# Ten steps of the samples' matrix memory ahead of the heads in place of eight, in a decoder step whose order is written out

## The chip, the cores and the metric

The kernel runs on one core of one Trainium2 chip. The metric is device time in microseconds (us) of one execution, lower is better; the median of the runs of the kernel before is 1042.33 us (1041.23 to 1043.42, three runs). The engines are TensorE (PE), with its weight loads shown apart as PEld, VectorE (DVE), ScalarE (ACT), GpSimd (POOL) and SyncE (SP), which issues nearly all transfers.

## The reference, cut to what matters

One step of a decoder trunk of two layers, in float32: 512 new tokens of a prompt and one new token for each of 8 samples share the weights. Layer 0 is a native sparse attention, layer 1 an mLSTM of 4 heads of width 512. The change concerns layer 1: its gate path z, and the part of the mLSTM that updates each sample's matrix memory C of 512 x 512, one for each of 8 samples and 4 heads, so 32 in all.

```python
# nsa layer: q, k, v, gates, z = h @ w_in; three branches (compressed, selected, window); out = (o * silu(z)) @ w_out
# mLSTM layer:
proj = h @ w_in
xm, z = proj[..., :D_INNER], proj[..., D_INNER:]          # D_INNER = 2048
c = jax.nn.silu(conv)                                      # conv of xm, width 4
q, k, v = block products of c and xm; ig, fl = gates of q, k, v
# per sample and head, one token:
num   = S @ v + decay * (q @ C)
den   = sum(S) + decay * (q . n)
hc    = num / max(|den|, exp(-mt))
C_new = carry_decay * C + w * outer(k, v)                  # 512 x 512, an output
hn    = hc * rsqrt(mean(hc * hc) + eps)
out   = (hn * norm_w + skip * c) * jax.nn.silu(z)
return x + out @ w_out
```

The prompt's 512 tokens go through the same cell, as one chunk of decay weights here.

## The kernel before, in words

The 520 tokens lie along the free axis and are worked in two column halves of 260. Every product in float32 is made as three products of rounded parts, high by high, high by low and low by high; so each weight tile is loaded (`wraw`), rounded to its high part (`whi`, on ACT or DVE) and subtracted to its low part (`wlo`, on DVE or POOL), before PE can use it.

By the time at which PE works on them, the stages of the profiled execution are: key, value and compression 0 to 207 us; q and z of layer 0 to 307; attention to 467; the product with W_o to 518; the xm half of layer 1's input product to 647; the zm stage, that is the z half, to 751; the heads to 996; the last output product and norm to 1036.

No scheduler decides the order. Each stage first registers its operations with their dependences, and then emits them in the sequence that a table of numbers gives: ORDER0 for the attention (934 operations), CALLS1 for the 712 recorded pieces of W_o and xm, ORDER1 for the zm stage (348 operations) and ORDER2 for the heads (933). Each engine runs what it is given strictly in that order. A second kind of table, MOVED1 for the pieces of CALLS1 and MOVEDP0 to MOVEDP2 for the other three, names operations that change engine: a copy between ACT and DVE, an elementwise operation between DVE and POOL. All instructions are emitted by one helper, so every row of the profile has its line, L504, and rows are told apart by the tiles they write and read.

The zm stage takes the 15 remaining of 16 weight tiles of z (`wraw<-in_m_in`, 512 KB each), one product for each half of the columns (24 matmuls `mm<-hhi,whi` and the like), its SiLU and a store (`zd<-zt`). Beside this it works out the prompt's gates, and runs the first eight steps of the samples' memory. A step k is sample k % 8 of head k // 8 (`state_step`):

- two loads of half a memory each (`cs<-in_state_C`, 512 KB);
- on PE the read of the old memory, 8 small matmuls `d<-cs,QZ`, gathered over the 8 samples of a head in one bank `d`, and one matmul `t<-VB,OH` that spreads the sample's v over the partitions;
- on ACT two multiplications by the decay (`cs<-cs,SBC`), on DVE four outer products added to it (`cs<-t,wk,cs`);
- two stores `o_cs<-cs`, 512 KB each.

Ahead of a head's first step `head_open` makes the samples' q for it (`QZ`), its rows and `VB`; after its eighth step `head_close` takes the denominators (`sd`, `dn`, `nm`), squares the result (`pr`) and sums the squares on PE with `t<-pr,ones`, and normalises it into `HN`. NZ says how many steps stand in the zm stage:

```python
    for ft in range(1, 16):
        zm_ops(P, ft, ZT * (ft - 1))
    gate_ops(P, GDUE)
    for k in range(NZ):
        state_step(P, k, ZS0 + ZSP * k)
    for n in range(2 * NZ, 2 * NZ + 4):
        state_load(P, n, ZT * 15 - 10)
    P.run(ORDER1, R, NE, MOVEDP1)
```

The remaining steps stand in the heads, among the prompt's heads: for each head the values v are split in high and low parts (`vh`, `vl`), q and k are made by block products (`mm<-CT,bdm`, `t<-bdk,ctw`), scores `s<-q,CT` follow, then the values, the head's norm (`acc`, `hx`, `hy`), the gating into `num`, its split in `uh` and `ul`, and 8 output products of 4 tiles each (`mm<-uh,whi` and the like, out_unit), each added to the residual `x`.

Of the kernel before, what the change touches and what calls it, by code (L numbers as in the profile page):

```python
# [55 lines left out]
ZT, ZS0, ZSP, NZ, GDUE = 6.4, 6.0, 11.0, 8, 8.0  # L56
# [52 lines left out]
)  # L109
ORDER1 = (  # L110
# [16 lines left out]
)  # L127
ORDER2 = (
# [173 lines left out]
MOVEDP1 = (7, 27, 31, 42, 46, 47, 61, 77, 82, 87, 91, 112, 117, 127, 132, 136, 162, 166, 167, 172, 177, 181, 182, 192,  # L302
    196, 197, 202, 211, 212, 248, 255,)
# [237 lines left out]
def step_kernel(ctx, tc, ap):  # L541
# [1409 lines left out]
    xm_val(15)  # L1951
    R.run(NE, CALLS1, MOVED1)
    mctx.close()
# [912 lines left out]
```

## Time and profile before

| | before |
|---|---|
| median of three runs | 1042.33 us |
| the profiled execution | 1037.7 us |
| its span | 1036.0 us |
| mean granted PE clock | 0.998 |
| PE busy | 1012.9 us, 98% of the span |
| DVE busy | 784.4 us, 76% |
| ACT busy | 532.7 us, 51% |
| POOL busy | 380.6 us, 37% |
| moved by DMA | 197.19 MB, mean 190 GB/s |

Busy time is the time in which an engine has an instruction in work. Matmuls overlap in PE's pipeline and their ends are modelled, so that a row's mean of 285 ns for a matmul of 260 columns is longer than the 0.12 us that lie between the starts of two. A wait is the idle time of an engine just before an instruction, put down to what released it. The profiled execution's own time is 4.6 us below the median of the runs shown.

### The profile page before, as it was taken

The numbers are of one execution on the slowest core, as the hardware profiler recorded it, in microseconds if no ns is written. First come the engines' busy times: TensorE is split into PE (matmuls) and PEld (weight loads), VectorE is DVE, ScalarE is ACT, GpSimd is POOL, SyncE is SP. The second block draws the span as 40 slices with busy tenths as digits, with TensorE's granted clock in tenths as the row PEclk, the third lists the DMA queues.
The fourth block names the chain that finished last, engine by engine and source line by source line (L and its number), as shares of the span: only waits on it lengthen the run. The fifth ranks groups of instructions, "written<-read, shape, count | busy, mean of one in ns | idle before, by whom it ended". The sixth has DMA issues, their size and how long they took to land.

```text
span 1036.0 us, 24026 instructions
## 1 busy us (share of the span) xinstructions
PE 1012.9 (98%) x8743; PEld 909.0 (88%) x8743; DVE 784.4 (76%) x1879; ACT 532.7 (51%) x1228; POOL 380.6 (37%) x430
## 2 busy tenths in 40 slices
PE   7999999999999999999999999999999999999998
PEld 6989999899998888779999998898857678877987
DVE  7876764568568987775887786866677888989885
ACT  5253342533268877761444455656655665463543
POOL 1072433301246656362234433332323335434330
PEclk9999999999999999999999999999999999999999
DMA  7664453133335624547434642688789789898543
GB/s 251 200 199 143 152 163 121 50 117 118 113 100 159 188 84 123 164 144 255 144 110 166 209 144 73 245 277 304 276 269 358 256 273 316 284 338 287 190 137 113
DMA packets 124793, 197.19 MB, mean 190 GB/s; under 512 B 16118, under 2 KB 66167, under 8 KB 124419
## 3 DMA queue, kind: packets, MB, share of 16 engines
q1 hardware_dynamic: 118866, 186.37, 54.7%
q10 hardware_dynamic: 5808, 9.28, 2.5%
q8 instruction: 69, 1.13, 0.4%
q14 instruction: 50, 0.40, 0.1%
HBM read 145.89 MB, written 58.10 MB: 197 GB/s over the span
## 4 chain that ended last, share of the span: by engine, by line
PE 67%; DVE 5%; ACT 2%; POOL 1%; issue 0%; DMA 0%; ACTq 0%; DVEq 0%
PE mm L504 44%; PE s L504 9%; PE t L504 8%; PE d L504 6%; ACT s L504 1%; DVE num L504 1%; DVE s L504 1%; POOL s L504 0%; DMA wraw<-in_m_in 0%; DVE ul L504 0%; DVE x L504 0%; ACT pt L504 0%; DVE wlo L504 0%; DVE hx L504 0%; DVE sc L504 0%
## 5 line engine op out<-in xcount | busy, mean ns | idle before, releaser
L504 PE MATMUL mm<-hhi,whi 128*128 128x260 f32 (+1 forms) x952 | 273.1, 287 | 0.9 <-ACT hhi L504 0.9
L504 PE MATMUL mm<-hhi,wlo 128*128 128x260 f32 (+1 forms) x952 | 269.9, 283 | 2.1 <-POOL wlo L504 1.1
L504 PE MATMUL mm<-hlo,whi 128*128 128x260 f32 (+1 forms) x952 | 269.6, 283 | 0.0
L504 PEld LDWEIGHTS mm<-hhi,whi 128*128 128x128 f32 (+1 forms) x952 | 178.4, 187 | 5.6 <-issue 3.6
L504 PEld LDWEIGHTS mm<-hhi,wlo 128*128 128x128 f32 (+1 forms) x952 | 178.3, 187 | 2.8 <-DVE wlo L504 1.5
L504 PEld LDWEIGHTS mm<-hlo,whi 128*128 128x128 f32 (+1 forms) x952 | 178.1, 187 | 0.8 <-DVE hlo L504 0.2
L504 POOL TENSOR_TENSOR wlo<-wraw,whi 128x1024 fp32r<-128x1024 f32 (+2 forms) x49 | 94.5, 1931 | 177.1 <-DVE whi L504 118.1
L504 DVE SCALAR_TENSOR_TENSOR cs<-t,wk,cs 128x512 f32<-128x512 f32 x128 | 89.1, 743 | 13.0 <-ACT cs L504 11.3
L504 ACT ACTIVATE cs<-cs,SBC 128x1024 f32<-128x1024 f32 x64 | 71.6, 1144 | 33.8 <-PE d L504 31.2
L504 POOL TENSOR_SCALAR s<-s,sm 128x256 f32<-128x256 f32 (+3 forms) x69 | 70.1, 1026 | 38.6 <-DVE sm L504 20.2
L504 ACT ACTIVATE s<-s,mn 128x256 f32<-128x256 f32 (+3 forms) x128 | 70.6, 554 | 16.8 <-DVE mn L504 12.8
L504 PE MATMUL s<-phi,w1h 128*128 128x256 f32 (+1 forms) x256 | 77.1, 301 | 0.0
L504 PE MATMUL s<-plo,w1h 128*128 128x256 f32 (+1 forms) x256 | 74.7, 292 | 2.3 <-DVE plo L504 2.3
L504 PE MATMUL s<-phi,w1l 128*128 128x256 f32 (+1 forms) x256 | 74.1, 289 | 0.0
L504 DVE TENSOR_TENSOR wlo<-wraw,whi 128x1024 fp32r<-128x1024 f32 (+1 forms) x53 | 61.1, 1154 | 9.2 <-ACT whi L504 4.5
L504 ACT ACTIVATE whi<-wraw 128x1024 fp32r<-128x1024 f32 (+1 forms) x53 | 46.7, 884 | 38.8 <-DMA wraw<-in_m_out 14.1
L504 PE MATMUL mm<-uh,whi 128*128 128x260 f32 x224 | 65.1, 291 | 0.0
L504 PE MATMUL mm<-uh,wlo 128*128 128x260 f32 x224 | 63.3, 282 | 1.5 <-DVE wlo L504 1.5
L504 DVE CUSTOM_DVE_ANT_0 s<-s,D 128x512 f32<-128x512 f32 (+3 forms) x128 | 57.8, 488 | 7.8 <-PE s L504 7.4
L504 PE MATMUL mm<-ul,whi 128*128 128x260 f32 x224 | 63.2, 282 | 0.0
L504 PEld LDWEIGHTS s<-plo,w1h 128*128 128x128 f32 x256 | 48.4, 189 | 4.0 <-DVE plo L504 2.8
L504 PEld LDWEIGHTS s<-phi,w1h 128*128 128x128 f32 x256 | 48.3, 189 | 0.6
(481 smaller groups left out, 2623.4 us busy)
## 6 DMA issues: line engine op xcount, KB each, us to landing
cs<-in_state_C SPq DMA_DIRECT2D x64, 512.0 KB, 6.5
o_cs<-cs SPq DMA_DIRECT2D x64, 512.0 KB, 5.0
praw<-in_cache SPq DMA_DIRECT2D x128, 128.0 KB, 3.0
dk<-in_cache SPq DMA_DIRECT2D x128, 128.0 KB, 2.6
wraw<-in_m_in SPq DMA_DIRECT2D x32, 512.0 KB, 4.0
wraw<-in_m_out SPq DMA_DIRECT2D x32, 256.0 KB, 4.9
wraw<-in_w_kv SPq DMA_DIRECT2D x11, 512.0 KB, 3.7
wraw<-in_w_q SPq DMA_DIRECT2D x8, 512.0 KB, 3.8
```

The costliest lines, as they stand in the source:

```text
L504: return f(*[real(x) for x in a], **{n: real(x) for n, x in k.items()})
```

## The change

NZ goes from 8 to 10. Steps 8 and 9, the first two samples of head 1, and with them the `head_open` of head 1, are registered in the zm stage and no longer in the heads: 25 operations, so that the zm stage has 373 and the heads 908. ORDER0, ORDER1, ORDER2 and CALLS1 are replaced as a whole, as are MOVED1 and MOVEDP0 to MOVEDP2; operations that change engine are 123 in place of 118 in the attention, 136 in place of 139 in W_o and xm, 38 in place of 31 in the zm stage and 111 in place of 116 in the heads. CALLS0, CALLS2, CALLS3 and their tables are as before. No operation is added or taken away.

```diff
--- before.py
+++ after.py
-ZT, ZS0, ZSP, NZ, GDUE = 6.4, 6.0, 11.0, 8, 8.0
+ZT, ZS0, ZSP, NZ, GDUE = 6.4, 6.0, 11.0, 10, 8.0
 ORDER0 = (
-    828, 792, 54, 55, 57, 834, 830, 8, 9, 108, 10, 11, 13, 14, 12, 71, 15, 37, 28, 793, 16, 17, 59, 60, 34, 61,
...
+    911, 830, 828, 792, 54, 55, 8, 13, 9, 10, 834, 11, 12, 71, 14, 15, 16, 17, 37, 28, 31, 61, 59, 57, 793, 18,
...
-MOVED1 = (20, 27, 29, 30, 36, 45, 52, 61, 62, 69, 71, 72, 73, 79, 88, 89, 95, 104, 112, 117, 126, 127, 152, 157, 164,
...
+MOVED1 = (27, 29, 30, 36, 45, 46, 59, 67, 68, 72, 73, 79, 88, 89, 95, 105, 117, 124, 126, 127, 147, 152, 157, 164,
...
-MOVEDP0 = (19, 20, 23, 24, 41, 47, 64, 65, 66, 67, 69, 84, 93, 95, 99, 119, 120, 123, 164, 166, 167, 184, 186, 190,
...
-MOVEDP1 = (7, 27, 31, 42, 46, 47, 61, 77, 82, 87, 91, 112, 117, 127, 132, 136, 162, 166, 167, 172, 177, 181, 182, 192,
...
-MOVEDP2 = (82, 94, 170, 177, 189, 265, 272, 284, 285, 286, 288, 292, 295, 309, 338, 346, 357, 362, 373, 387, 388, 389,
...
+MOVEDP0 = (7, 19, 20, 23, 24, 41, 47, 50, 64, 66, 69, 84, 86, 89, 93, 95, 98, 99, 119, 120, 124, 164, 167, 184, 186,
...
+MOVEDP1 = (1, 12, 16, 22, 32, 42, 52, 57, 62, 76, 77, 82, 87, 92, 97, 102, 106, 117, 121, 127, 136, 142, 147, 152,
...
+MOVEDP2 = (57, 145, 152, 240, 247, 257, 258, 262, 263, 267, 282, 291, 294, 296, 313, 321, 322, 326, 332, 336, 337,
...
```

First place: PE where the zm stage ends and the heads begin. `t<-sd,ncs`, `t<-pr,ones` and `t<-cst,lse` belong to the closing of head 0 and to the gates, `d<-cs,QZ` and `t<-VB,OH` to steps of the memory, `mm<-CT,bdm` to the prompt's q. Before:

```order
L504 MATMUL mm<-hhi_9105,wlo 128x260
L504 MATMUL t<-sd,ncs 32x8 x16
L504 MATMUL t<-pr,ones 32x64 x4
L504 MATMUL t<-cst,lse 128x128 x4
L504 MATMUL t<-pr,ones 32x32 x4
L504 MATMUL t<-cst,VS 8x128 x4
L504 MATMUL mm<-CT_9799,bdm 128x512
L504 MATMUL mm<-CT_9898,bdm 128x512
L504 MATMUL mm<-CT_9950,bdm 128x512
L504 MATMUL d<-cs,QZ_10218 32x512 x8
```

The changed kernel, in the same place:

```order
L504 MATMUL mm<-hlo_9193,whi 128x260
L504 MATMUL mm<-hhi_9072,wlo 128x260
L504 MATMUL t<-VB,OH 128x512
L504 MATMUL d<-cs,QZ_9877 32x512 x4
L504 MATMUL t<-cst,lse 128x128 x4
L504 MATMUL t<-VB,OH 128x512
L504 MATMUL t<-pr,ones 32x32 x4
L504 MATMUL t<-VB,OH 128x512 x2
L504 MATMUL d<-cs,QZ_9877 32x512 x4
L504 MATMUL mm<-CT_9799,bdm 128x512
L504 MATMUL mm<-CT_9724,bdm 128x512
```

The sums `t<-sd,ncs` and `t<-pr,ones` 32x64 now stand some 100 instructions further up (outside the piece), ahead of the last four half tiles of z; `t<-pr,ones` 32x32 has the memory read of step 9 and two spreads around it, and the block products of q come behind two more spreads and the read of step 10. The read that follows `mm<-CT,bdm` before is that of step 8, which now stands inside the last tile of z.

The same place on DVE, from the denominators `dn` and `nm` of head 0 over `pr` to the sum of squares `dn<-t` and the factor `hf_v`; `zt` is the SiLU of z. Before:

```order
L504 TENSOR_TENSOR zt<-mm,rr_9636 128x260
L504 TENSOR_REDUCE dn<-t 128x16
L504 TENSOR_TENSOR dn<-dn,SBC 128x16
L504 TENSOR_TENSOR dn<-dn 128x8
L504 TENSOR_TENSOR zt<-zt,zsg_12598 128x260
L504 TENSOR_TENSOR dn<-dn,SBC 128x8
L504 RECIPROCAL dn<-dn 128x8
L504 TENSOR_TENSOR nm<-VS,dn 128x32
L504 TENSOR_TENSOR nm<-nm,t 128x32
L504 TENSOR_TENSOR pr<-nm 128x32
L504 TENSOR_REDUCE dn<-t 128x8
L504 TENSOR_TENSOR hf_v<-dn 128x8
```

The changed kernel:

```order
L504 TENSOR_TENSOR nm<-VS,dn 128x32
L504 TENSOR_TENSOR nm<-nm,t 128x32
L504 TENSOR_TENSOR pr<-nm 128x32
L504 TENSOR_TENSOR zt<-zt,zsg_12517 128x260
L504 TENSOR_TENSOR zt<-zt,zsg_12559 128x260
L504 TENSOR_TENSOR zt<-mm,rr_9555 128x260
L504 TENSOR_TENSOR zt<-mm,rr_9632 128x260
L504 SCALAR_TENSOR_TENSOR cs<-t,wk,cs 128x512 x8
L504 TENSOR_REDUCE dn<-t 128x8
L504 TENSOR_TENSOR hf_v<-dn 128x8
L504 TENSOR_TENSOR hf_v<-hf_v,dn 128x8
```

`pr` came directly before the sum of its squares; now four rows of the SiLU and the eight outer products of steps 8 and 9, in one row here, stand between them.

Second place: the transfers that SP issues at the start of the zm stage, in this order (the numbers are those of the tiles). Before:

```order
L504 DMA wraw_11303<-in_m_in 128x1024
L504 DMA wraw_11334<-in_m_in 128x1024
L504 DMA wraw_11342<-in_m_in 128x1024
L504 DMA cs_11346<-in_state_C 128x2x512
L504 DMA cs_11391<-in_state_C 128x2x512
L504 DMA cs_11456<-in_state_C 128x2x512
L504 DMA zd_8938<-zt_11406 128x512
L504 DMA wraw_11518<-in_m_in 128x1024
```

The changed kernel:

```order
L504 DMA wraw_11310<-in_m_in 128x1024
L504 DMA wraw_11325<-in_m_in 128x1024
L504 DMA wraw_11356<-in_m_in 128x1024
L504 DMA cs_11358<-in_state_C 128x2x512
L504 DMA wraw_11373<-in_m_in 128x1024
L504 DMA cs_11443<-in_state_C 128x2x512
L504 DMA cs_11450<-in_state_C 128x2x512
L504 DMA wraw_11452<-in_m_in 128x1024
L504 DMA cs_11494<-in_state_C 128x2x512
```

Three weight tiles are still issued ahead of the first memory loads; the fourth (`wraw_11373`) now comes next and serves z tile 5, and the fifth (`wraw_11452`) serves tile 4, whose product comes first. Its buffer is that of `whi` of tile 2, which PE has to have read before.

Third place: DVE in the last of the four heads, where the head's norm ends and the gating begins. `hx<-t,hx` reads the head's sum of squares from PE, `num` is the gating, `x<-x,mm` the residual of an output product, `cs<-t,wk,cs` an outer product of the last steps. Before:

```order
L504 TENSOR_TENSOR pr<-nm 128x32
L504 TENSOR_TENSOR x_13211<-x_13211,mm 128x260 x2
L504 SCALAR_TENSOR_TENSOR hx<-t,hx 128x512
L504 TENSOR_REDUCE dn<-t 128x8
L504 TENSOR_TENSOR hf_v<-dn 128x8
L504 TENSOR_TENSOR hf_v<-hf_v,dn 128x8
L504 TENSOR_SCALAR hf_v<-hf_v 128x8
L504 TENSOR_TENSOR x_14009<-x_14009,mm 128x260
L504 TENSOR_TENSOR hx<-hx,hy 128x512 x2
L504 SCALAR_TENSOR_TENSOR hy<-hx,hy 128x512
L504 TENSOR_TENSOR wlo<-wraw,whi 128x512
```

The changed kernel:

```order
L504 SCALAR_TENSOR_TENSOR hx<-hx,ab 128x512
L504 TENSOR_TENSOR acc<-acc,sq_15208 128x512
L504 TENSOR_TENSOR wlo<-wraw,whi 128x512
L504 CAST whi<-wraw 128x512
L504 SCALAR_TENSOR_TENSOR cs<-t,wk,cs 128x512 x2
L504 SCALAR_TENSOR_TENSOR hx<-t,hx 128x512
L504 TENSOR_TENSOR x_13682<-x_13682,mm 128x260 x2
L504 TENSOR_REDUCE dn<-t 128x8
L504 TENSOR_TENSOR hf_v<-dn 128x8
L504 TENSOR_TENSOR hf_v<-hf_v,dn 128x8
L504 TENSOR_SCALAR hf_v<-hf_v 128x8
L504 TENSOR_TENSOR hx<-hx,hy 128x512 x2
```

A row of the sum `acc`, two of weight splits and two outer products now stand directly ahead of `hx<-t,hx`.

More of the change, by code (lines that the diff above doesn't have):

```diff
@@ L295 @@
 MOVED3 = (2, 12, 16, 23, 30, 31, 35, 42, 65, 69, 103, 120, 124, 136, 141,)
-MOVEDP0 = (19, 20, 23, 24, 41, 47, 64, 65, 66, 67, 69, 84, 93, 95, 99, 119, 120, 123, 164, 166, 167, 184, 186, 190,
[5 rows of a table removed]
-MOVEDP1 = (7, 27, 31, 42, 46, 47, 61, 77, 82, 87, 91, 112, 117, 127, 132, 136, 162, 166, 167, 172, 177, 181, 182, 192,
-    196, 197, 202, 211, 212, 248, 255,)
-MOVEDP2 = (82, 94, 170, 177, 189, 265, 272, 284, 285, 286, 288, 292, 295, 309, 338, 346, 357, 362, 373, 387, 388, 389,
[5 rows of a table removed]
+MOVEDP0 = (7, 19, 20, 23, 24, 41, 47, 50, 64, 66, 69, 84, 86, 89, 93, 95, 98, 99, 119, 120, 124, 164, 167, 184, 186,
[5 rows of a table added]
+MOVEDP1 = (1, 12, 16, 22, 32, 42, 52, 57, 62, 76, 77, 82, 87, 92, 97, 102, 106, 117, 121, 127, 136, 142, 147, 152,
+    157, 162, 177, 182, 187, 192, 211, 212, 222, 225, 230, 246, 248, 328,)
+MOVEDP2 = (57, 145, 152, 240, 247, 257, 258, 262, 263, 267, 282, 291, 294, 296, 313, 321, 322, 326, 332, 336, 337,
[5 rows of a table added]
 LATE = ((3, 1), (3, 2), (3, 3))
```

302 rows, old and new, of tables (CALLS1, MOVED1, MOVEDP0, MOVEDP2) are left out of this document.

## The prediction

> **What bounds the kernel now.** I read the busy times by stage first, then the waits of PE, then the chain of waits and the timelines at the two ends of the moved work. The busy times of each engine in the attention, the zm stage and the heads (columns: PE, PEld, DVE, ACT, POOL, each with its count, then the granted clock, the DMA engines' share and GB/s):
>
> ```profile
> 307.00:467.00 160.00, 159.01 (x1902) 132.19 (x1899) 131.81 (x517) 122.00 (x377) 92.14 (x107) 0.99 0.48 143
> 647.00:751.00 104.00, 101.70 (x858) 92.72 (x851) 73.77 (x134) 62.61 (x119) 33.23 (x40) 1.00 0.79 276
> 751.00:996.00 245.00, 242.74 (x1748) 188.71 (x1746) 211.63 (x463) 131.44 (x221) 91.66 (x102) 1.00 0.83 282
> ```
>
> PE is busy for 101.70 of 104 us in the zm stage and 242.74 of 245 in the heads, at full clock. So PE bounds both, and since the change adds and removes no matmul, the time can fall only by what PE waits for. All the waits of PE that matter (us in total, times, longest):
>
> ```profile
> PE s L504 <- ACT sq L504: 5.5, 1, 5.5
> PE mm L504 <- DVE wlo L504: 2.5, 2, 1.5
> PE t L504 <- DVE pr L504: 2.1, 1, 2.1
> PE d L504 <- DVE QZ L504: 0.4, 1, 0.4
> PE s L504 <- DVE ul L504: 0.4, 1, 0.4
> ```
>
> The first is in a stage that stays as it is; so is one of the two in the second row (the other, 1.5 us, is in the last head, its row below). That leaves 2.1 + 0.4 around the end of the zm stage and 1.5 + 0.4 in the last head, 4.4 us in all, of which the first two are where the steps move. PE's timeline there (start, duration, then in brackets the wait and its releaser):
>
> ```profile
> 747.94 0.66 PE L504 MATMUL t<-cst,lse 128*128 128x128 f32 x4
> 750.65 0.27 PE L504 MATMUL t<-pr,ones 128*32 128x32 f32 x8 [2.05 <-DVE pr L504]
> 751.28 2.74 PE L504 MATMUL mm<-CT,bdm 128*128 128x512 f32 x6
> 754.47 1.99 PE L504 MATMUL d<-cs,QZ 128*32 128x512 f32 x16 [0.44 <-DVE QZ L504]
> 756.83 2.32 PE L504 MATMUL s<-q,CT 128*128 128x512 f32 x8
> ```
>
> and DVE's, from the first row of head 0's closing to the last that PE waits for:
>
> ```profile
> 748.06 0.23 DVE L504 TENSOR_REDUCE dn<-t 128x16 f32<-128x64 f32 x1
> 750.40 0.19 DVE L504 TENSOR_TENSOR pr<-nm 128x32 f32<-128x32 f32 x1
> 754.10 0.38 DVE L504 COPY QZ<-QKS 128x8 f32<-128x8 f32 x4
> ```
>
> The closing of head 0 starts when the last product of z is done, so its nine small rows on DVE, from 748.06 to 750.59, lie bare: PE has nothing else until `pr`. Then the rest of the closing delays `QZ` of head 1, and the read of step 8 waits.
>
> **The change, part by part.** *Steps 8 and 9 and the opening of head 1 go to the zm stage.* What one step takes on the engines, from the groups of the zm stage (busy, mean ns):
>
> ```profile
> L504 DVE SCALAR_TENSOR_TENSOR cs<-t,wk,cs 128x512 f32<-128x512 f32 x32 | 22.4, 742 | 4.6 <-ACT cs L504 4.6
> L504 ACT ACTIVATE cs<-cs,SBC 128x1024 f32<-128x1024 f32 x16 | 17.8, 1140 | 9.6 <-PE d L504 9.6
> L504 POOL TENSOR_TENSOR wlo<-wraw,whi 128x1024 fp32r<-128x1024 f32 x6 | 14.5, 2413 | 21.7 <-DVE whi L504 11.8 <-ACT whi L504 6.6 <-PE mm L504 3.3
> L504 DVE CAST whi<-wraw 128x1024 fp32r<-128x1024 f32 x9 | 6.7, 747 | 0.9 <-DMA wraw<-in_m_in 0.9
> ```
>
> Two steps move 8 outers x 0.742 = 5.9 us of DVE, 4 scalings x 1.14 = 4.6 us of ACT and, by the timeline (1.99 us for 16 reads), 2.0 us of PE with two spreads of some 0.3 more. DVE goes to about 80 of 104 us in the zm stage and 206 of 245 in the heads, ACT to 67 and 127: neither becomes the bound. PE's share merely changes places. By itself this part is worth nothing.
>
> *The boundary.* Now the first sums of head 0's closing stand four half tiles of z earlier on PE (some 11 us at 0.12 us a matmul), and the nine rows on DVE run under those products, so the 2.05 us go. `QZ` of head 1 is made within the stage, under products too, so the 0.44 us go as well. What is late next: DVE ends the stage with eight outers in a row, 5.9 us, then the factor and `q<-mm`. PE has meanwhile a read, three spreads, the sum, another read (1.0 each) and four block products at 0.46 (2.74 for six), together about 7.3 us by these rows, before it needs a bank that an outer frees after some 6.5 us, and scores after 9.5 us that need `q`, due on DVE at 9.4. I put 0.2 us for these. Ends: 0, and 2.0 if DVE starts its eight outers late by the 1.8 us of ahead-lying SiLU rows.
>
> *The start of the zm stage.* The chain of waits there (start, us, what):
>
> ```profile
> 644.52 3.96 DMA wraw<-in_m_in
> 648.51 1.07 ACT whi L504
> 649.60 1.24 DVE wlo L504
> 650.88 9.18 PE mm L504 x74
> ```
>
> PE has other work meanwhile: of the stage's 2.3 idle us (104 less 101.70) 2.05 are the wait for `pr`, so some 0.25 can show here. `whi` of the first tile moves from ACT (1.07) to DVE (0.747 by the group), which shortens the chain by 0.3. I take -0.2; ends -0.3 and 0.
>
> *The weights in the zm stage.* Tile 4 of z is now loaded after tile 5 and into a buffer that PE frees with its last read of tile 2; before its own product PE has only tile 3 (48 matmuls x 0.12 = 5.8 us) and about 2.9 us of memory steps and spreads, 8.7 us. The way of the weight: issue, landing, `whi` on ACT 1.07, `wlo` on POOL 2.41. Issues of that stage with the us to landing, and the fullest pieces of stage and heads:
>
> ```profile
> cs<-in_state_C SPq DMA_DIRECT2D x18, 512.0 KB, 6.4
> wraw<-in_m_in SPq DMA_DIRECT2D x15, 512.0 KB, 4.2
> 690.00:710.00 20.00, 20.00 (x160) 17.61 (x159) 15.46 (x25) 10.48 (x22) 7.03 (x8) 1.00 0.92 311
> 900.00:930.00 30.00, 30.00 (x274) 23.64 (x273) 24.73 (x62) 16.76 (x31) 11.10 (x9) 1.00 0.98 338
> ```
>
> With the median of 4.2 the way is 7.7 us and hidden with 1.0 to spare; with a landing like that of a memory load, 6.4, it is 9.9 and PE waits 1.2. ACT has scalings of 1.14 queued in between, which uses up the spare. I take 0.5; ends 0 and 2.3 (a scaling more on top of 6.4). SP issues in order: behind that weight wait two loads, stores of `o_cs` and the next weight, which shifts them, not PE, as long as tile 5 lies loaded already. The other tiles have two products, over 11 us, ahead of them, and stay covered.
>
> *The transfers.* Eight of 512 KB, 4.2 MB, come to the zm stage: 104 us x 276 GB/s = 28.7 MB become 32.9 MB, 316 GB/s. The heads show 338 GB/s over 30 us at a DMA share of 0.98 with PE at 30.00 of 30, so I cost it at 0; the bound above is in the rivals. The Trainium skill ("DMA: Bandwidth & Descriptors", Specifications) names about 358 GB/s as the limit of one core at HBM; that is 92 us for 32.9 MB, an estimate by that page, and leaves the term at 0 as well.
>
> *The last head.* Rows of DVE where its norm ends, PE's wait behind it, the group of `num<-num,zs` (shortest, median and longest in ns), and POOL:
>
> ```profile
> 971.84 0.74 DVE L504 SCALAR_TENSOR_TENSOR cs<-t,wk,cs 128x512 f32<-128x512 f32 x1
> 974.29 0.69 DVE L504 SCALAR_TENSOR_TENSOR hx<-t,hx 128x512 f32<-128x512 f32 x1 [0.22 <-PE t L504]
> 975.71 0.42 DVE L504 TENSOR_TENSOR x<-x,mm 128x260 f32<-128x260 f32 x1
> 978.40 0.69 DVE L504 TENSOR_TENSOR wlo<-wraw,whi 128x512 fp32r<-128x512 f32 x1
> 981.78 1.78 DVE L504 TENSOR_TENSOR num<-num,zs 128x512 f32<-128x512 f32 x1
> 990.69 0.39 PE L504 MATMUL mm<-uh,wlo 128*128 128x260 f32 x1 [1.55 <-DVE wlo L504]
> L504 DVE TENSOR_TENSOR num<-num,zs x8: 677/684/1780, 823.8 to 991.5; 128x512 f32<-128x512 f32 x8
> 971.24 1.30 POOL L504 TENSOR_TENSOR acc<-acc,sq 128x512 f32<-128x512 f32 x1 [1.28 <-ACT sq L504]
> 981.32 1.70 POOL L504 TENSOR_TENSOR wlo<-wraw,whi 128x512 fp32r<-128x512 f32 x1 [5.95 <-ACT whi L504]
> ```
>
> From 974.29 DVE works without a gap until the last `ul`, and PE, with twelve products to do, runs dry for the 1.5 + 0.4 us. Before, `hx<-t,hx` comes 1.75 us after the last `acc` (971.24 + 1.30). In the changed order `acc` is on DVE (0.68, as an addition of that size takes there, in place of 1.30), but a split (0.69), a rounding (half of the 0.747 of a tile twice as wide) and two outers (1.48) stand between it and `hx`: 2.6 us, and one addition to `x` more (0.42) lies behind. That is -0.6 + 0.8 + 0.4 = +0.6, less what earlier starts of this head give; I take +0.5. Ends: -1.0 (half of the 1.9 us goes) and +2.0 (the split waits for its weight as well).
>
> A row of that fence bears on a rule: the `num<-num,zs` that started under POOL's split took 1.78 us, and the median of the group is 0.684. The Trainium skill ("SBUF — State Buffer", Who interferes with whom) says that a DVE instruction with two inputs in SBUF and a GpSimd instruction that reads SBUF exclude each other for the whole of the first. The trace agrees: 1.78 is the rest of POOL's row (to 983.02) and then the addition. By the rule the tail would be an estimated 1.1 shorter if no split on POOL meets an addition in the new order; as five splits still follow on POOL, I don't count it.
>
> *Attention, W_o and xm* are re-ordered. The waits of PE that the attention shows, and the largest of its weight loads:
>
> ```profile
> PE t L504 <- DVE dxo L504: 0.2, 1, 0.2
> PE d L504 <- ACT pt L504: 0.2, 1, 0.2
> PEld t L504 <- ACT pt L504: 1.9, 5, 0.5
> ```
>
> There are four such rows of PE of 0.2, 0.8 us, and the loads lie mostly under matmuls. I take 0; ends -0.8 (all go) and +1.5 (three new waits like the longest loads', 0.5 each).
>
> *Sum:* -2.05 - 0.44 + 0.2 - 0.2 + 0.5 + 0.5 + 0 = -1.5 us on the profiled execution's 1037.7 (its span of 1036.0 and 1.7 around it), so 1036.2 there. That run stands 4.6 below the median of the runs shown; taken from the median, 1042.3 - 1.5 = 1040.8.
>
> **The rivals.** *The whole gain* (1037.8 to 1039.6): weights stay covered, and the last head and the attention lose nothing: -2.5 - 0.2, with up to -1.0 and -0.8 more, is -2.7 to -4.5, about 1038.7. For it speaks that every row of before hides a weight in the zm stage but for its start; against it the two outers and the split ahead of `hx`.
>
> *The wait only changes its name* (1041.7 to 1043.5): PE waits for the eight outers or `q` instead of for `pr`, by the 2.0 of the upper end, and the rest of the sum, +0.8, takes what is left: -2.5 + 2.0 + 0.8 = +0.3, about 1042.6. For it speaks that DVE has 11 us of rows in line at the boundary; against, that none of these is asked for before 6.5 us.
>
> *Slower* (1044.5 to 1046.5): landings in the fuller zm stage become those of the slowest memory loads, so that `wraw` comes at over 7 us. Then tile 4 costs 2.3 and a second tile, held in SP's line behind it, as much again: -1.5 - 0.5 + 2 x 2.3 = +2.6, about 1044.9, more with a third. It decides from a landing of about 6.5 us on. For it speaks the share of 0.92 that 20 us of the stage show already at 311 GB/s, and 316 would be the mean of the stage; against, the 338 GB/s of the heads without a wait of PE.
>
> **How the numbers follow.** The forecast's own case (1039.6 to 1041.7) has 0.42, the whole gain 0.22, the new name 0.15, slower 0.21. A measurement of this kernel tells about 0.2%, 2.1 us, from no change: faster means below 1040.2, slower above 1044.4. Of the first case I count 0.17 below 1040.2, so faster has 0.22 + 0.17 = 0.39, same 0.25 + 0.15 = 0.40, slower 0.21. The range of 1037.8 to 1045.0 holds the first three cases but for their thin ends (0.05) and the slower case up to about its two late tiles; 0.12 lies above.
>
> **What would show it.** In the profile after: no wait for `pr` and none for `QZ` near 750, and the four block products directly behind a read of memory; if a wait for `cs` or `q` stands there, the new name was right. A wait `mm <- POOL wlo` in the first 25 us of the zm stage, of 0 to 2.3 us, is tile 4's. The stage should show a DMA share of about 0.88 and 310 to 320 GB/s, and loads of `wraw` at 4 to 5 us; 7 would be the slower case. In the last head the wait for `wlo` or `ul` of PE should add up to 2.4 where it was 1.9. The prediction is wrong if the attention gains or loses over 1.5 us, for which the waits of before give no ground.

## The result and the profile after

The changed kernel takes 1052.69 us (median, 1052.32 to 1052.87), the kernel before 1042.88 us in the same comparison: a ratio of 1.0099, 95% interval 1.0080 to 1.0119. It is slower by some 10 us, where the prediction said 1040.8 and a range up to 1045.0. The profiled execution after has 1052.87 us, close to its median; that of before had 1037.7, so the two profiles differ by 15.2 us, of which 4.6 are the fast execution of before.

Where PE's rows put the stages (start of the row named, us; worked out from the two timelines, differences before rounding):

| up to | before | after | stage is longer by |
|---|---|---|---|
| first `d<-dk,QZ` (stages that stay as they are) | 263.8 | 267.2 | 3.4 |
| last `mm<-uo,whi` (attention, W_o) | 513.0 | 516.4 | 0.0 |
| last `s<-xm,FG` (xm) | 646.6 | 657.3 | 7.4 |
| first `mm<-CT,bdm` (zm) | 751.3 | 763.1 | 1.1 |
| first `s<-uh,whi` (heads) | 995.1 | 1010.6 | 3.6 |
| end | 1036.0 | 1051.2 | -0.3 |

The zm stage now holds, ahead of the first `mm<-CT,bdm`, three reads of the memory (1.0 each) and four spreads (0.4 each) that came later before, 4.6 us of PE; it is only 1.1 longer, so it gained 3.5. The heads lost the same 4.6 us of work and are 3.6 longer: they lost 8. And the xm half lost 7.4 without any work added. In the xm half and in the heads, one stretch of half clock on PE, worth 1.7 us each time, is part of the loss; the last section shows them.

Of PE's waits after, the largest and those on which the argument rests (total, times, longest). Left out are the others of the stages ahead of the attention, which before has in nearly the same size, a new one of 0.8 us in the attention (`ACT dpt`), and those under 0.5:

```profile
PE s L504 <- ACT sq L504: 5.6, 1, 5.6
PE mm L504 <- DVE wlo L504: 3.0, 2, 2.0
PE t L504 <- DVE cs L504: 2.8, 1, 2.8
PE mm L504 <- DVE xm L504: 2.0, 2, 1.0
PE d L504 <- ACT QKS L504: 1.7, 2, 1.2
PE t L504 <- DVE cwn L504: 1.0, 2, 0.6
PE s L504 <- DVE ul L504: 0.7, 1, 0.7
PE d L504 <- DMA cs<-in_state_C: 0.5, 1, 0.5
PE d L504 <- POOL bd L504: 0.5, 1, 0.5
```

`DVE pr` (2.1) and `DVE QZ` (0.4) are gone, as forecast. In the xm half `xm`, `QKS` and `bd` are new, 4.2 us; in the heads `cs` and `cwn` and the load of `cs` are new, 4.3 us, and `wlo` and `ul` are 0.8 more.

The wait for `cs` is the largest of those that before doesn't have. DVE, SP and PE around it, in the changed kernel:

```profile
799.27 1.40 DVE L504 SCALAR_TENSOR_TENSOR cs<-t,wk,cs 128x512 f32<-128x512 f32 x2
801.19 1.41 DVE L504 SCALAR_TENSOR_TENSOR cs<-t,wk,cs 128x512 f32<-128x512 f32 x2
800.74 2.29 SPq L504 DMA_DIRECT2D o_cs<-cs  x3
803.13 0.69 SPq L504 DMA_DIRECT2D wb<-rd  x1
809.90 0.69 DVE L504 CUSTOM_DVE_ANT_0 ctw<-CT,wb 128x512 f32<-128x512 f32 x1 [3.56 <-DMA wb<-rd]
813.62 2.71 DVE L504 SCALAR_TENSOR_TENSOR cs<-t,wk,cs 128x512 f32<-128x512 f32 x4
816.39 0.60 PE L504 MATMUL t<-cst,VS 128*8 128x128 f32 x4 [2.84 <-DVE cs L504]
```

Read upward from PE: its product needs a bank that the outer products free; DVE does these at 813.62, after `ctw`, which stood idle for 3.56 us until the row `wb` of the prompt's head 2 had landed; and SP issued that row at 803.13, behind three stores of the memory: it had stood 7.36 us ahead of the first, until the outer products of 799.27 were done, and another 0.94 us ahead of the third, for those of 801.19. DVE's waits for `wb` in all, in the changed kernel and then in the kernel before (profiled again):

```profile
  DMA wb<-rd: 8.1, 3
```

```profile
  PE mm L504: 0.3, 1
```

The second has no `wb` at all: there these rows are ordered early enough. Of the three rows in the first, those of heads 1 and 2 stand behind stores that wait for DVE; that of head 0 goes out when its own source (`rd<-rows`) has landed, which in turn was issued behind such a store.

### The profile page after: what moved, and what is told of

The parts are those of the page before. It is cut to its first block, busy times and chain, and to the rows that moved or that the text cites. A ratio compares the mean times of both kernels' runs of the same rounds, so it can differ in the third digit from the quotient of the medians.

```text
span 1051.2 us, 24051 instructions
## 1 busy us (share of the span) xinstructions
PE 1020.6 (97%) x8743; PEld 913.6 (87%) x8743; DVE 783.0 (74%) x1849; ACT 541.8 (52%) x1247; POOL 386.9 (37%) x441
## 4 chain that ended last, share of the span: by engine, by line
PE 57%; DVE 9%; DMA 5%; ACT 3%; issue 1%; POOL 1%; SPq 0%; ACTq 0%; DVEq 0%; POOLq 0%
PE mm L504 37%; PE s L504 8%; PE t L504 6%; PE d L504 5%; DMA cs<-in_state_C 2%; DVE cs L504 1%; DMA wb<-rd 1%; DVE num L504 1%; DMA o_cs<-cs 1%; ACT s L504 1%; DMA wraw<-in_m_out 1%; DVE cva L504 0%; DVE s L504 0%; POOL s L504 0%; DVE x L504 0%
## 5 line engine op out<-in xcount | busy, mean ns | idle before, releaser
L504 PEld LDWEIGHTS mm<-hhi,wlo 128*128 128x128 f32 (+1 forms) x952 | 180.5, 190 | 2.5 <-POOL wlo L504 1.3
L504 PEld LDWEIGHTS mm<-hlo,whi 128*128 128x128 f32 (+1 forms) x952 | 180.3, 189 | 0.6 <-DVE hlo L504 0.2
L504 POOL TENSOR_SCALAR s<-s,sm 128x128 f32<-128x128 f32 (+3 forms) x67 | 70.1, 1056 | 43.8 <-DVE sm L504 17.0
L504 ACT ACTIVATE whi<-wraw 128x1024 fp32r<-128x1024 f32 (+1 forms) x62 | 54.6, 887 | 51.6 <-PE mm L504 17.1
L504 ACT ACTIVATE s<-s,mn 128x384 f32<-128x384 f32 (+3 forms) x128 | 70.7, 555 | 16.3 <-DVE mn L504 9.8
L504 DVE CUSTOM_DVE_ANT_0 s<-s,D 128x128 f32<-128x128 f32 (+3 forms) x128 | 56.7, 485 | 6.9 <-PE s L504 5.9
```

The source lines that it names most:

```text
L504: return f(*[real(x) for x in a], **{n: real(x) for n, x in k.items()})
```

## The experiments

Every kernel was timed against the kernel before; the ratio has its 95% interval.

| kernel | us, median | ratio to before |
|---|---|---|
| ctrl (before, again) | 1041.9 | 1.0000 (0.9988 to 1.0013) |
| att_only | 1042.4 | 0.9997 (0.9981 to 1.0012) |
| xm_only | 1047.0 | 1.0047 (1.0032 to 1.0063) |
| zh_only | 1049.4 | 1.0068 (1.0051 to 1.0084) |
| xm_fix | 1044.2 | 1.0016 (1.0000 to 1.0032) |
| wb_early | 1044.2 | 1.0013 (0.9992 to 1.0034) |
| mixed | 1047.3 | 1.0047 (1.0028 to 1.0066) |
| after_mended | 1044.9 | 1.0029 (1.0017 to 1.0042) |
| wb_late | 1041.9 | 0.9990 (0.9973 to 1.0007) |
| best | 1053.9 | 1.0106 (1.0080 to 1.0132) |
| best2 | 1045.0 | 1.0020 (0.9999 to 1.0040) |
| before_tail | 1042.5 | 1.0001 (0.9981 to 1.0022) |

**Which part.** The first four kernels take one part of the change each.

ctrl: no edit.

> The kernel before, unchanged, profiled once more. The profile of before that the prediction used (1037.7 us) lies 4.6 us under the median of its runs and shows one stretch of lowered PE clock before its last stage (380 to 400 us, 1.8 us lost); the changed kernel's shows five (0.83 to 0.87 in one slice of 10 us each, some 1.7 us each). Theory A (the change costs by new waits): this run takes about 1042.5 us and shows three or more such stretches, so the clock explains the 4.6 us between the two executions of before and little of the step to 1052.7. Theory B (the change costs by the clock): it shows one or two, at about 1042 us.

1041.9 us, and its profile has one stretch of lowered clock, not three: theory B's count. So the clock is not what separates these two executions of before, and a part of the step to 1052.7 may be the clock's. More on this at the end. Against the profile of before, its stages ahead of the attention are 1.9 us longer and its heads 2.0, with a wait of 1.4 for `Sl` that was 0.2 there: single profiles of one kernel differ by that much.

att_only:

```diff
-ORDER0, MOVEDP0 of before
+ORDER0, MOVEDP0 of the changed kernel
```

> Only the attention's order and engine changes (ORDER0, MOVEDP0) are the changed kernel's. Theory A: 0, since from the first read of the attention to the last W_o product both profiles take the same time to 0.1 us (249.2 us): within 1 us of before. The prediction's bounds were -0.8 to +1.5. Rival (the attention changes where the clock drops later): +2 or more, with one more lowered stretch.

No difference, as forecast. Single waits came and went (`ACT dpt` 0.8 is new), below what the timing tells.

xm_only:

```diff
-CALLS1, MOVED1 of before
+CALLS1, MOVED1 of the changed kernel
```

> Only the order and the engine changes of W_o and xm (CALLS1, MOVED1) are the changed kernel's. Theory A, new waits: PE waits 2.0 us for xm, 1.7 for QKS, 0.5 for bd there in the changed kernel and for none of them before: +4 to +6 us, 1046.5 to 1048.5. Rival (the loss is in the heads, and what the xm half shows is the clock's): within 1.5 us of before. Rival B, the clock: any difference goes with the number of lowered stretches.

+4.9 us by its ratio: theory A, and half of the whole loss. In its profile the xm half takes 139.5 us where ctrl has 134.0; of these 5.5 us, 2.9 are PE's waits beyond ctrl's and 1.7 a stretch of half clock that follows the wait for `xm`.

zh_only:

```diff
-NZ = 8; ORDER1, ORDER2, MOVEDP1, MOVEDP2 of before
+NZ = 10; ORDER1, ORDER2, MOVEDP1, MOVEDP2 of the changed kernel
```

> Only NZ, the zm stage's and the heads' orders and engine changes (NZ, ORDER1, ORDER2, MOVEDP1, MOVEDP2) are the changed kernel's; the attention, W_o and xm are as before. Theory A: the zm stage gains about 2 us at its end (no wait for pr and QZ), the heads lose 4 to 6 (PE waits 2.8 for cs, 1.0 for cwn, 0.5 for a load of cs, more before small matmuls): +2 to +5 us, 1044.5 to 1047.5. Rival, the prediction's own sum (the loss is all in W_o, xm and the clock): -1.5 us.

+7.1 us, somewhat above theory A's range. Against ctrl its zm stage is 2.3 us longer with 4.6 us of PE more, so it gains 2.3; its heads, from the first `mm<-CT,bdm` to the first `s<-uh,whi`, take 248.8 us in place of 245.8 with 4.6 less. 7.6 us are lost there: 4.8 in new or longer waits of PE (3.1 `cs`, 1.0 `cwn`, 0.6 `cs` load, 0.5 `wlo`, less 0.4 for `QZ`), 1.7 in a stretch of half clock that follows the wait for `wlo`, and 1.1 that I can't assign.

The three effects add up to 12, the whole change to 10; within the intervals that is one sum.

**What in xm.** Two of PE's waits in xm_only, each with the rows that lead to it, first the wait for `xm`, then the longer one for `QKS`:

```profile
617.53 1.06 ACT L504 ACTIVATE whi<-wraw 128x1024 fp32r<-128x1024 f32 x1 [3.83 <-PE mm L504]
618.50 0.16 ACT L504 ACTIVATE VS<-d 128x8 f32<-128x8 f32 x1
618.69 0.17 DVE L504 COPY QKS<-d 128x16 f32<-128x16 f32 x1 [2.64 <-ACT VS L504]
620.35 0.42 DVE L504 TENSOR_TENSOR xm<-mm,rr 128x260 f32<-128x260 f32 x1
620.82 0.39 PE L504 MATMUL mm<-hhi,whi 128*128 128x260 f32 x1 [1.00 <-DVE xm L504]
568.48 0.69 DVE L504 CAST whi<-wraw 128x1024 fp32r<-128x1024 f32 x1 [1.66 <-PE mm L504]
569.29 0.16 DVE L504 COPY VS<-d 128x8 f32<-128x8 f32 x1
569.54 0.18 ACT L504 ACTIVATE QKS<-d 128x16 f32<-128x16 f32 x1 [5.41 <-DVE VS L504]
569.78 0.61 PE L504 MATMUL d<-CT,bd 128*128 128x8 f32 x4 [1.21 <-ACT QKS L504]
```

In the first, ACT stands 3.83 us at a rounding whose buffer PE has not freed; a copy of 0.16 us is behind it; DVE waits 2.64 us for that copy, with the additions of finished products behind it in its order; and PE then has no bank. The second is the same pattern with the engines exchanged: DVE stands 1.66 us at a rounding whose buffer PE has not freed, the copy `VS<-d` is behind it, and `QKS<-d` on ACT, idle for 5.41 us, waits for that copy, and PE for `QKS`. The other wait for `QKS`, 0.44 us, is for a copy that stands behind SiLUs on ACT. Of the two copies, the tables moved one to ACT anew. The changed kernel has one more wait for `xm`, of 0.96 us, that no row here follows.

xm_fix, against xm_only:

```diff
 CALLS1 = (
-    ... 595, 518, ...
+    ... 518, 595, ...
-MOVED1 = (... 326, ... 421, ...)
+MOVED1 = (... without 326 and 421 ...)
```

> As xm_only (1047.0 us), but with one ACT instruction one place later (a rounding of a weight, whi<-wraw, that waits 3.8 us for its buffer, now behind the copy VS<-d that stood behind it) and two copies QKS<-d on DVE in place of ACT. Theory E (in-order ACT: what waits there for PE or for DVE holds small copies that PE's next small products need): PE's waits for xm (1.0) and QKS (1.7 in two) go, time 1044 to 1045.5. Rival (DVE is what is late and the waits come back under another name): within 1 us of xm_only.

1044.2 us: about two thirds of the loss came back, 0.47% falling to 0.16%, with one instruction set one place later and two copies on DVE. The waits for `xm` (1.0) and `bd` (0.5) went. That for `QKS` hardly did: with the copy on DVE it stands behind the same rounding on DVE, which still waits 1.66 us, and PE waits 1.11 in place of 1.21. With `ACT VT` 0.4 and `DVE xm` 0.3, 1.8 of the 3.2 us of waits in the xm half came back or stayed, so the rival had the larger part in the waits. The xm half takes 136.7 us in place of 139.5, and of these 2.8 us 1.7 are the stretch of half clock, which is not there any more. The three edits were made together; the rows speak for the one on ACT.

**What in the heads.** wb_early, against zh_only, moves two transfers:

```diff
 ORDER2 = (
-    ... 307, 11, 385, 308, ...       (wb of head 1)
-    ... 340, 341, 505, 342, ...      (wb of head 2)
+    ... 2, 3, 385, 4, ...
+    ... 319, 304, 505, 7, ...
```

> As zh_only (1049.4 us), but two small transfers stand earlier on SP: the row loads wb<-rd of heads 1 and 2 of the prompt, of heads 1 ahead of one and of head 2 ahead of five or more stores and loads of the memory. Theory D (SP issues the row behind stores that wait for DVE, DVE waits for the row in order, and its outers free PE's bank late): DVE's waits for wb go from 8.1 us in 3 to under 2, PE's wait of 3.1 us for cs goes, and the time falls by 2 to 4 us, to 1045.5 to 1047.5. Rival (the transfers are slow since the DMA engines are full, 6 us from issue to landing whenever they are issued): PE's wait for cs moves and stays over 2 us, time within 1 us of zh_only.

1044.2 us, 5 to 6 us back from two small transfers, more than forecast. PE's wait for `cs` is gone, DVE waits for `wb` only for head 0. In the profile the heads take 243.2 us in place of 248.8: 3.1 for `cs`, 1.1 for `Sl` and 1.7 of half clock have gone. Its timeline, SP and then DVE (the line of the helper is L499 here, since this kernel's tables take fewer lines):

```profile
766.21 0.32 SPq L499 DMA_DIRECT2D wb<-rd  x1
778.55 0.34 SPq L499 DMA_DIRECT2D wb<-rd  x1
793.56 2.28 SPq L499 DMA_DIRECT2D o_cs<-cs  x3
799.08 0.69 DVE L499 CUSTOM_DVE_ANT_0 ctw<-CT,wb 128x512 f32<-128x512 f32 x1
```

DVE's waits for `wb` in all (total, times), in wb_early:

```profile
  DMA wb<-rd: 2.6, 1
```

The row of head 2, which zh_only issues at 799.63 behind three stores, now goes out at 778.55, ahead of them, and `ctw` runs at 799.08 without a wait; in zh_only it ran at 806.70 after one of 3.85. Theory D holds. The rival does not: the row landed 3.4 us after its issue.

mixed: the zm stage of the change, the heads in the order of before without the 25 operations that moved.

```diff
-NZ = 8; ORDER1, MOVEDP1 of before
+NZ = 10; ORDER1, MOVEDP1 of the changed kernel
-ORDER2, MOVEDP2: 933 operations
+ORDER2, MOVEDP2: the same sequence without operations 0 to 22, 31 and 32 (908, renumbered)
```

> NZ is 10 and the zm stage has the changed kernel's order and engine changes; the heads have the order and engine changes of before, with the 25 operations that moved taken out and nothing else altered; attention, W_o and xm are as before. Theory C (the move is good, the restated order of the heads lost the time): the zm stage keeps its gain of about 1.6 us and the heads lose nothing, so 1039.5 to 1041.5, within or a little under before. Rival (the move itself starves the heads, which have fewer steps to put between): PE waits for cs or cwn in the heads again, 1044 or more.

1047.3 us: the rival. The heads of before open with filler between `bdm`, `q` and `ctw`, namely the reads of steps 8 and 9; without them PE waits 2.1 for `q`, where the 2.0 us of reads stood, and further 2.0 for `bdm` and 2.0 for `cwn` in the first 20 us, and DVE 4.7 for head 0's `wb`; the granted clock is at half for 10.2 us from 761.4 on. So the move needs an order of the heads of its own, and theory C fails: the restated order is not the only cause. How much of the loss is the missing filler is not shown, since head 0's `wb`, behind which `cwn` stands, is late on SP here too: its source `rd<-rows` is issued behind a store that waits for the outer products at the end of the zm stage.

after_mended: the changed kernel with the edits of xm_fix and wb_early and nothing else.

> The changed kernel with the edits of wb_early and xm_fix together: in the heads two small transfers wb<-rd earlier on SP, in the xm half one ACT instruction one place later and two copies on DVE; nothing else of the change is altered. If these four places are what the change lost (theory C and E together), 6 of the 7 us of the heads and 4 of the 5 of xm come back: 0.5 to 2.5 us above before, so 1043 to 1045.5. Rival (the losses hide others, which show once these are gone): over 1047.

1044.9 us, 0.29% above before where the change was 0.99% above it: seven of the ten microseconds hang on these five edits, two transfers, one rounding and two copies. The 3 us left are not settled; 2.0 for `wlo` in the last head, 0.9 for `cwn`, 1.9 for loads of `cs` and 1.1 for `QKS` are the waits that before doesn't have in that size.

wb_late, the converse in the kernel before:

```diff
 ORDER2 = (
-    ... 411, 29, 530, 348, ...
+    ... 586, 412, 530, 531, ...      (59 places later)
```

> The kernel before with one instruction moved: the row load wb<-rd of the prompt's head 2 stands 13 operations ahead of its first use on DVE, as in the changed kernel, in place of 72 ahead. Theory D: DVE waits 3 us or more for it where it waits for none before, and PE 1 to 4 us: 1044 to 1047. Rival (in the heads of before DVE has slack at that place, and the load alone does no harm): within 1 us of before.

No harm at all. At its late place the store ahead of the row on SP waits only 0.7 us for DVE, the row goes out at 785.13, and `ctw` uses it at 792.22 without a wait. In the changed kernel SP stood over 8 us at the stores ahead of the same row. So a late place in the order was not enough here; how long the line ahead of it waits made the difference.

best, against wb_early:

```diff
 ORDER2 = (
-    ... 872, 245, 824, ... 896, 246)
+    ... 844, 245, 246, 906, ...)       (246 is its store)
```

> wb_early (0.9 us above before), and in the last head one outer product (cs<-t,wk,cs, two instructions of 0.74 us, whose store nobody waits for) stands behind the last split ul<-num,uh in place of directly ahead of hx<-t,hx; attention, W_o and xm as before. The prediction's term for the last head: what stands ahead of hx there delays the gating, and PE runs dry at the end (2.05 for wlo and 0.7 for ul in wb_early, 1.5 and 0.4 in before). Expected: these 2.75 fall to 1.3 or less, time 1042 to 1043, at or under before. Rival (DVE is late there by its sum, and the order within does not matter): within 0.5 us of wb_early.

1053.9 us, far off, and by the same mechanism that I had just seen. SP's rows:

```profile
988.83 14.67 SPq L499 DMA_DIRECT2D o_cs<-cs  x2
1003.61 5.29 SPq L499 DMA_DIRECT2D wraw<-in_m_out  x8
```

And PE's waits in the last 30 us before 1015 (total, times, longest):

```profile
PE mm L499 <- DVE wlo L499: 1.0, 1, 1.0
PE s L499 <- ACT whi L499: 7.3, 1, 7.3
```

The aim was reached: the wait for `wlo` fell from 2.05 to 1.0. But "nobody waits for the store" was wrong: SP's two stores take 14.67 us, the second waiting for the late outer product, and eight weight loads of the last stage stood behind it, the first issued 14 us later than in wb_early (989.32) and the last 11. PE waited 7.3 us for one of them, and the granted clock was 0.50 from 1004.7 to 1014.9, so that the last matmuls ran slower as well. This is the converse that wb_late was meant to be: a store that waits, with loads behind it, is enough to cost 10 us.

best2 and before_tail, subtractions of the last head on POOL:

```diff
 best2, against wb_early:     MOVEDP2 without 878, with 864 and 892
 before_tail, against before: MOVEDP2 without 903, with 917
```

> wb_early (0.9 us above before), and in the last head three of the subtractions wlo<-wraw,whi on POOL in place of DVE, each while POOL is idle. Theory: PE's wait of 2.05 for wlo there comes from DVE, which has 27 us of rows in line, so that the split comes 2.8 us after its high part; on POOL it comes within 1.3 us and the wait goes; DVE has 2.1 us less: -1.5 to -2.5 us against wb_early, 1040.5 to 1041.8, under before. Rival (what POOL reads holds up DVE's additions by the same amount, as the 1.78 us row showed): within 0.7 us of wb_early.

> The kernel before with two of those subtractions of the last head on POOL in place of DVE, nothing else. By the same theory PE's waits of 1.5 (wlo) and 0.4 (ul) go: -1 to -1.9 us against before. Rival: within 0.7 us of before, with one addition more on DVE that takes over 1 us.

Neither is faster; no version here beats the kernel before clear of its interval. The rival holds. In the last head, DVE's rows of 128x512 that take over 1 us, where 0.68 to 0.75 is usual, are two in before and three in before_tail, and three in wb_early and five in best2, each while a subtraction of a weight runs on POOL. The wait for `wlo` did go in both, and another took its place at the next step:

```profile
997.84 2.05 PE L505 MATMUL t<-bdk,ctw 128*128 128x128 f32 x16 [0.84 <-POOL bdk L505]
1002.98 0.39 PE L505 MATMUL s<-ul,whi 128*128 128x260 f32 x1 [0.42 <-DVE ul L505]
```

(before_tail; in best2 it is 2.2 us for `x`.) I read this so: DVE's sum sets the end of the last head, and a wait of PE ahead of it is only where PE spends the time that it has over. No run shows that by itself.

## Why the prediction was wrong, by its own steps

- *The boundary:* right. `pr` and `QZ` are gone, no wait for `q`, and the zm stage gained 2.3 us in zh_only and 3.5 in the changed kernel's profile; the sum had -2.05 - 0.44 + 0.2. The working behind the 0.2 does not come out, though: the rows it names for PE add up to 5.0 us and not to 7.3 (5.7 were measured, from the first read at 759.32 to the end of the fourth block product), so that `q` came in time not by that margin, but because PE had eight block products in line, not four, and ACT, not DVE, took the first copy of `q` at 766.06. That part is luck.
- *The start of the zm stage and tile 4:* no wait of PE for a weight is in that stage after, though `wraw` landed in 5.1 us at the median in place of 4.2. The term of 0.5 was 0.
- *The transfers:* the cost of 0 in the zm stage was right, at a lower load than forecast (288 GB/s at a share of 0.84 over 657 to 763 us; I had put 316 and 0.88). The failure was not bandwidth: the median landing of `wb<-rd` is 5.5 us in the changed kernel and 5.7 in before, profiled again.
- *The last head:* PE's waits for `wlo` and `ul` are 2.7 us, where 2.4 was said.
- *Attention:* 0, as said.
- *W_o and xm: this step failed.* It stood in one line with the attention, and its ends of -0.8 and +1.5 were taken from waits of the attention. The order of these 712 pieces was not followed at all; measured +4.9, in waits for `xm`, `QKS` and `bd` and a stretch of half clock, where 0 was put. The row that speaks for the danger was in the profile of before: PE busy 128.81 of 129 us in the xm half, a stage whose new order can hardly gain.

```profile
518.00:647.00 129.00, 128.81 (x1154) 125.03 (x1156) 96.73 (x211) 61.46 (x140) 49.95 (x67) 1.00 0.42 139
```

- *The heads between boundary and last head: no term at all, and this step failed too.* The prediction asked of SP's order only in the zm stage, "which shifts them, not PE". In the heads the same question had the answer of zh_only: rows `wb<-rd` behind stores, 8.1 us of waiting on DVE, and 7.6 us lost in the stage, of which two of these rows, set earlier, brought 5 to 6 back. The rival "slower" had the right line (SP's) and the wrong stage and transfer.
- *The fill that moved away:* the prediction called moving the steps "by itself worth nothing". mixed shows +5 with the heads' old order: steps 8 and 9 were what PE did while DVE and POOL prepared head 0. How much of the 5 is theirs stays open, since `wb` is late there as well.

## What the runs showed of the clock

PE's granted clock in slices of one microsecond around the wait for `QKS` in the changed kernel (PE, PEld, DVE, ACT, POOL, then the clock):

```profile
569.00:570.00 1.00, 0.69 (x6) 0.47 (x4) 0.40 (x1) 0.00 (x0) 0.00 (x0) 1.00 0.00 0
570.00:571.00 1.00, 0.10 (x1) 0.10 (x1) 1.00 (x5) 0.34 (x3) 0.00 (x0) 1.00 0.00 0
571.00:572.00 1.00, 1.00 (x8) 1.00 (x9) 0.96 (x2) 0.09 (x2) 0.63 (x2) 0.85 0.00 0
572.00:573.00 1.00, 1.00 (x7) 1.00 (x6) 0.52 (x2) 0.59 (x1) 1.00 (x1) 0.50 0.00 0
574.00:575.00 1.00, 1.00 (x7) 1.00 (x6) 0.00 (x0) 0.00 (x0) 0.84 (x2) 0.50 0.00 0
575.00:576.00 1.00, 1.00 (x10) 1.00 (x10) 0.00 (x0) 0.00 (x0) 0.00 (x0) 0.95 0.00 0
...
817.00:818.00 1.00, 1.00 (x8) 0.08 (x8) 1.00 (x3) 0.00 (x0) 0.92 (x1) 0.73 0.33 127
818.00:819.00 1.00, 1.00 (x5) 0.50 (x2) 1.00 (x2) 0.07 (x1) 0.35 (x1) 0.50 0.00 0
```

I had not expected this: about a microsecond after a wait of 1.2 us, PE ran at half clock for 3.4 us (0.85, then 0.50, back at 575), and the same after the wait of 2.84 at 816. At half clock 3.4 us of matmuls lose 1.7, an estimate from these rows, so such a wait can cost more than twice itself. xm_only shows it after its wait at 620.82, zh_only after the wait for `wlo`. It does not follow every wait: the same wait of 2.05 for `pr` stands in seven of the profiles, and a stretch of half clock begins within 1.5 us of its end in three of them (xm_only, xm_fix, before_tail) and in the other four not (before, ctrl, att_only, wb_late). Nor is it tied to new waits alone: the stretches at 77 and 207 us, in stages that are the same in all kernels, are there in the changed kernel's profile and not in ctrl's; these two are the 3.4 us of the first row of the stage table. The Trainium skill ("TensorE: Matmul & The Clock Gate", What's actually happening) tells of a gate that passes half the pulses after an idle window of about 3.4 us, in windows that run freely. The 0.50, the length of 3.4 us and the chance in it agree; the idle time does not: 1.2 us without matmuls was enough here.

In the timed runs the mean granted clock is 0.995 for before (ctrl and its partner), 0.994 for xm_only, 0.993 for zh_only and 0.992 for the changed kernel. A line with one slope for ctrl, its partner, xm_only and zh_only gives 0.58 us for each 0.001; over the runs of all kernels of the table it is 0.88. By these, some 1.7 to 2.6 of the 10 us go with the clock; the rest is waiting and what I could not assign. Since several of the stretches follow waits, the two are not independent: of what xm_fix and wb_early won in their stages, 1.7 us each was such a stretch.

## What to carry to other kernels

Where engines run in a written order, follow each queue that issues transfers through every stage that was re-ordered, and ask of each waiting store which loads stand behind it: here two rows of 256 KB behind waiting stores cost 5 to 6 us, and one outer product set later, whose store then held the line, cost 10. When a stage has the bounding engine busy 99.8% of the time, a new order of it has next to nothing to gain, and "0" is the good end of the range, not its middle. Work that is moved to fill one gap leaves another where it was filling; look at what the bounding engine does in those microseconds before calling the move free.
